# A decoder layer's first token block: read from a transposed copy of x, and finer first conditioning chunks

## The chip, the cores and the metric

The kernel runs on one core of a Trainium2 chip. The metric is the device time of one execution in microseconds, the median of three runs. A core has five engines with a queue of instructions each: TensorE (PE: matmuls, with weight loads PEld beside them), VectorE (DVE), ScalarE (ACT), GpSimd (POOL) and SyncE (SP), which here issues the DMA transfers. Each engine works through its own queue in order and waits at an instruction until what it needs is there.

## The reference

One hybrid decoder layer over 2048 tokens of width 1024, conditioned by a vector c:

```python
mod = jax.nn.silu(c) @ w_ada + b_ada
sh1, sc1, ga1, sh2, sc2, ga2 = jnp.split(mod, 6, axis=-1)
h = modulate(rms_norm(x, g_attn), sh1, sc1)          # x/rms * g * (1 + sc1) + sh1
x = x + ga1[:, None, :] * hybrid_mixer(h, w_in, b_f, sinks, w_out)
h2 = modulate(rms_norm(x, g_mlp), sh2, sc2)
x = x + ga2[:, None, :] * conv_glu_mlp(h2, w_up, conv_w, conv_b, w_down)
return rms_norm(x, g_final)
```

The mixer multiplies h by w_in (q, k, v of a sliding-window group and of a forgetting-attention group, and its gate logits), runs both attentions, and multiplies by w_out. What matters here is the first line and the first part of the third: before anything can be multiplied by w_in, the shift sh1 and the scale sc1 (each 1024 numbers) must come out of `silu(c) @ w_ada`, and x must be divided by its root mean square.

## The kernel before

Tokens are taken in four blocks of 512. For each block there are stages: s1 (h and the input projection), s2 (attention) and s3 (output projection and MLP). Precision: each float32 operand is split into a high and a low part of a reduced format (hh and hl for h, wh and wl for a weight, line 384 and 385 make the latter), and each product is three matmuls, wh·hh, wh·hl and wl·hh. h is held transposed: tile k has 128 of the 1024 features on the partitions and 512 tokens along the row, k from 0 to 7.

The first block has a prologue of its own, since weights, conditioning and x all arrive at the same time.
- `prep(0)` (lines 562 to 577) loads x in rows, four tiles of 128 tokens in two halves of 512 features (line 510). ScalarE sums the squares (line 491), GpSimd forms the inverse root (lines 495 and 496), VectorE scales the rows (line 568).
- `first_groups` (from line 242) first transposes the scaled rows with TensorE (line 517) and copies each of the eight transposed tiles out of PSUM (line 252).
- The conditioning is computed in four chunks of 256 shift and 256 scale columns, enough for two k each. A chunk is eight tiles of w_ada of 128x512, loaded at line 200; VectorE multiplies each by an entry of silu(c) and adds it up (lines 205 and 207). `shape` then sums over the partitions with small matmuls against ones (line 262) and forms shift and scale (lines 267 to 269).
- `modulate_one` makes h for one k: ScalarE applies scale and shift (line 525), ScalarE rounds to hh (line 115), VectorE takes hl (line 530).
- `products` (line 282) multiplies: seven groups of 128 output columns (four q groups, accumulators "d", and three k groups, accumulators "acc") are accumulated over all eight k, three matmuls each, so 21 matmuls for one k and 168 in all. The weights come as sets: for each pair of k one set for the q groups (128x1024) and one for the k groups (128x768), eight sets, numbered 0 to 7. `feed(loads, splits)` issues loads up to a number (line 425) and splits sets up to a number. From inside `products` it runs ahead and reaches sets 8 and 9, which belong to what follows the block. Weight tiles raw, high and low share ten buffers.
- `store_group` (lines 583 to 586) writes the finished groups to memory; the loads of sets 10 and 11 are issued ahead of it by code that stands behind it.

What sets the order: the kernel is written in a language whose planner orders each engine's instructions by priority (program order) and by its own simulated clock, and puts in all waits. Around `first_groups` the order of VectorE and SP is written by hand: those instructions keep their program order among themselves, though instructions from outside can be planned in between. TensorE and ScalarE are ordered by the planner. The loop in `first_groups` is woven: while chunk i is being summed on VectorE, chunk i-1 is shaped after the second step and its two k are modulated and multiplied between later steps; the products with the k groups are put off until the next chunk's column sum has been issued.

Of the kernel before, what the change touches and what calls it, by code (L numbers as in the profile page):

```python
# [8 lines left out]
F32 = mybir.dt.float32  # L9
F32R = mybir.dt.float32r  # L10
BF16 = mybir.dt.bfloat16
AF = mybir.ActivationFunctionType
ALU = mybir.AluOpType
AX = mybir.AxisListType

P = 128
D = 1024
S = 2048
TB = 512
NB = S // TB  # L20
KT = D // P
# [4 lines left out]
EPS = 1e-6  # L26
BIG = 1e30
NT = 10
# [23 lines left out]
MMB = 1  # L52
# [19 lines left out]
def tile_decoder_layer(  # L72
    ctx: ExitStack,
    tc: tile.TileContext,
    x: bass.AP,
    c: bass.AP,
    w_ada: bass.AP,
    b_ada: bass.AP,
    g_attn: bass.AP,
    w_in_c: bass.AP,  # L80
# [45 lines left out]
    def side_ps(w=512):  # L126
        t = pa.tile([P, 512], F32, tag="s", name="sd", bufs=3)
        return t[:, :w]
# [59 lines left out]
    def ada_chunk(i, accs):  # L188
        acc = ap.tile([P, 512], F32, tag="act", name="acc")
        for k in range(KT):  # L190
            w = ap.tile([P, 512], F32, tag="act", name="wada")
            with behind():
                nc.sync.dma_start(w, w_ada[i, k])
            ada_step(acc, w, k)
            yield
        accs.append(acc)

    def ada_pair(i, k, acc):
        w = at.tile([P, 2, 256], F32, tag="t", name="wada2", bufs=NT)
        nc.sync.dma_start(w, w_ada[i, k].rearrange("p (s n) -> p s n", s=2))  # L200
        ada_step(acc, w.rearrange("p s n -> p (s n)"), k)

    def ada_step(acc, w, k):
        if k == 0:
            nc.vector.tensor_scalar(acc, w, cc[:, 0:1], 1.0, ALU.mult, ALU.mult)
        else:
            nc.vector.scalar_tensor_tensor(
                acc, w, cc[:, k : k + 1], acc, ALU.mult, ALU.add
            )
# [30 lines left out]
    late = {}  # L240

    def first_groups():
        rows = ready.pop(0)
        xts = []
        for k in range(KT):
            if k % 4 == 2:
                ps = pa.tile([P, 512], F32, tag="o", name="o0")
            else:
                ps = side_ps()
            transposes(ps, rows, k)  # L250
            xt = ap.tile([P, TB], F32, tag="act", name="xt")
            nc.scalar.copy(xt, ps)
            xts.append(xt)
        hh, hl = {}, {}
        acc = [dense_ps() for _ in range(4)]
        for tag, bufs in (("s", 3), ("o", 1), ("s", 3))[:FG]:
            acc.append(pa.tile([P, 512], F32, tag=tag, name="acc0", bufs=bufs))

        def shape(i, a):
            ps = side_ps(4)  # L260
            for j in range(4):
                nc.tensor.matmul(
                    ps[:, j : j + 1], a[:, j * P : (j + 1) * P], ones[:, 0:1],
                    start=True, stop=True,
                )
            js, jc = slice(2 * i, 2 * i + 2), slice(KT + 2 * i, KT + 2 * i + 2)
            nc.vector.tensor_add(mod[:, js], ps[:, 0:2], bada[:, js])
            nc.vector.tensor_add(mod[:, jc], ps[:, 2:4], bada[:, jc])
            nc.vector.scalar_tensor_tensor(
                scl[:, js], mod[:, jc], 1.0, gat[:, js], ALU.add, ALU.mult  # L270
            )

        def products(k, sets):
            a = k % 2
            for m in sets:
                i = NW * (k // 2) + m
                feed(i + 3, i + 2)
                wh, wl = parts[i]
                for g in range(4 * m, min(4 * m + 4, len(acc))):
                    gs = slice((g - 4 * m) * P, (g - 4 * m + 1) * P)  # L280
                    for j, (l, r) in enumerate(((wh, hh), (wh, hl), (wl, hh))):
                        nc.tensor.matmul(  # L282
                            acc[g], l[:, a, gs], r[k],
                            start=(k == 0 and j == 0), stop=(k == KT - 1 and j == 2),
                        )
                if a == 1:
                    parts.pop(i)
                    flow["used"] += 1

        prev = None  # L290
        for i in range(5):
            sums = None
            if i < 4:
                sums = ap.tile([P, 512], F32, tag="act", name="acc")
            for k in range(KT):
                if i < 4:
                    ada_pair(i, k, sums)
                if i > 0 and k == 1:
                    shape(i - 1, prev)
                    if i > 1:  # L300
                        for m in range(1, NW):
                            products(2 * i - 4, [m])
                            products(2 * i - 3, [m])
                if i > 0 and k in (3, 5):
                    kk = 2 * (i - 1) + (k - 3) // 2
                    modulate_one(*h_pair(hh, hl, kk), xts[kk], kk, 0, 0)
                    if k == 5:
                        products(kk - 1, [0])
                        products(kk, [0])
            prev = sums  # L310
            if i == 0:
                feed(3, 2)
        for m in range(1, NW):
            products(KT - 2, [m])
            products(KT - 1, [m])
        small_loads()
        for g in range(4):
            store_group(acc[g], q_d[0], 512 + g * P, 0.125)
        for g in range(FG):
            store_group(acc[4 + g], k_d[0], P + g * P, 1.0)  # L320
        return hh, hl

    def prologue_late():
        srcs = [(g_mlp, KT, "gml")]
# [90 lines left out]
    def feed(loads, splits):  # L415
        while flow["loaded"] < min(loads, len(reqs)):
            i = flow["loaded"]
            shape, srcs = reqs[i]
            key, use = mode.get(i, (None, "raw"))
            if use == "load":  # L420
                load_kept(i, shape, key)
            else:
                raws[i] = wp.tile(shape, F32, tag="w", name="wr", bufs=WS)
                for dst, src in srcs:
                    flow["last"] = nc.sync.dma_start(raws[i][dst], src).ins
            flow["loaded"] += 1
        while flow["split"] < min(splits, len(reqs)):
            i = flow["split"]
            key, use = mode.get(i, (None, "raw"))
            if use != "load":  # L430
                parts[i] = split_w(raws.pop(i), reqs[i][0])
                if use == "store":
                    store_kept(parts[i], reqs[i][0], key)
            flow["split"] += 1
# [80 lines left out]
    def transposes(ps, rows, k):  # L515
        for t, row in enumerate(rows):
            nc.tensor.transpose(
                ps[:, t * P : (t + 1) * P],
                row[k // 4][:, (k % 4) * P : (k % 4 + 1) * P], ident,
            )  # L520
        return ps
# [51 lines left out]
    def prep(n):  # L573
        for t in range(4):
            prep_tile(n, t)
# [925 lines left out]
    c_raw = columns_load(c.rearrange("o (k p) -> (o k) p", p=P), KT)  # L1501
    b_raw = columns_load(b_ada.rearrange("(k p) -> k p", p=P), 48)
    g_raw = columns_load(g_attn.rearrange("(k p) -> k p", p=P), KT)
    prep(0)
    cc = columns(None, KT, "cc", c_raw)
    ce = cp.tile([P, KT], F32, tag="ce", name="ce")
    nc.scalar.activation(ce, cc, AF.Exp, scale=-1.0)
# [20 lines left out]
def _laid_out(inputs, np):  # L1528


    def columns(w):
        return w.reshape(KT, P, -1, P).transpose(2, 1, 0, 3)

    def rows(w):
        return w.reshape(-1, 2, P, 2, 512).transpose(3, 0, 2, 1, 4)

    def head(w):
        return w.reshape(KT // 2, 2, P, -1).transpose(0, 2, 1, 3)

    def by_partition(w):  # L1540
        return w.reshape(KT, P, -1).transpose(1, 0, 2)

    out = {}
    for name in _INS:
        a = np.asarray(inputs[name])
        if name == "w_ada":
            first = a[:, : 2 * D].reshape(KT, P, 2, 4, 256).transpose(3, 0, 1, 2, 4)
            rest = a[:, 2 * D :].reshape(KT, P, 8, 512).transpose(2, 0, 1, 3)
            out[name] = np.concatenate([first.reshape(4, KT, P, 512), rest])
        elif name == "w_in":  # L1550
            out["w_in_c"] = columns(np.concatenate([a[:, :640], a[:, 768:1792]], axis=1))
            out["w_in_v0"] = by_partition(np.concatenate([a[:, 640:768], a[:, 1792:1984]], axis=1))
            out["w_in_v1"] = by_partition(a[:, 1984:2312])
            out["w_in_h0"] = head(a[:, 768:1280])
            out["w_in_h1"] = head(a[:, 1280 : 1280 + FG * P])
        elif name in ("w_out", "w_down"):
            out[name] = rows(a)
        elif name == "w_up":
            out[name] = columns(a)
        else:  # L1560
            out[name] = a
    return {name: np.ascontiguousarray(a) for name, a in out.items()}
# [29 lines left out]
```

## Time and profile before

| | us |
|---|---|
| Median of three runs | 2652.85 |
| Lowest, highest run | 2644.81, 2661.91 |
| Profiled execution, its own time | 2654.82 |
| Its span | 2653.1 |
| TensorE matmul, busy | 2542.7 (96%) |
| Weight loads, busy | 2152.4 (81%) |
| VectorE, busy | 1927.9 (73%) |
| ScalarE, busy | 1457.2 (55%) |

The profile is of one execution. A row of instructions gives its start, its busy time, engine, line of the kernel, operation and tiles, and in brackets the idle time before it and what ended it. "PEclk" and "granted clock" are the share of TensorE's full clock in a stretch. A row of the chain of waits gives start, length and what the chain passes through. A group's row gives its busy time, the mean ns of one, and idle time before it.

### The profile page before, as it was taken

How to read it: one execution, taken by the hardware profiler on the slowest of the kernel's cores; microseconds unless marked ns; L12 is line 12 of the kernel's file. 1: busy time of each engine (PE TensorE's matmuls, PEld its weight loads, DVE VectorE, ACT ScalarE, POOL GpSimd, SP SyncE). 2: the span in 40 equal slices, each digit the busy share in tenths (PEclk: the TensorE clock that was granted, in tenths of full speed). 3: DMA queues.
4: the chain of work that ended last, by engine and by line, in shares of the span. 5: the costliest groups of instructions: out<-in, count | busy, mean ns of one | idle time of the engine just before them, and what ended most of it. 6: DMA issues, size and time to landing. Idle time of an engine off the chain costs nothing.

```text
span 2653.1 us, 38432 instructions
## 1 busy us (share of the span) xinstructions
PE 2542.7 (96%) x12852; PEld 2152.4 (81%) x12852; DVE 1927.9 (73%) x3837; ACT 1457.2 (55%) x3061; POOL 86.1 (3%) x171
## 2 busy tenths in 40 slices
PE   7999989799999999999999999899998999999998
PEld 6888888688887889888888878788787778888887
DVE  6468767889898668788888767888888876344433
ACT  4456664655657676575556665755555665311222
POOL 0001000100000010010000000100000000000000
PEclk9999999799999999999999999999999999999999
DMA  6967679576556876756666799365554467655564
GB/s 230 302 205 251 198 217 331 204 243 205 192 182 224 274 255 215 257 193 246 226 231 235 255 300 320 126 202 184 185 168 144 160 225 260 238 192 190 191 235 177
DMA packets 304770, 588.25 MB, mean 222 GB/s; under 512 B 32188, under 2 KB 137396, under 8 KB 304572
## 3 DMA queue, kind: packets, MB, share of 16 engines
q1 hardware_dynamic: 304572, 585.79, 66.0%
q8 instruction: 102, 1.67, 0.3%
q14 instruction: 96, 0.79, 0.1%
HBM read 440.95 MB, written 144.71 MB: 221 GB/s over the span
## 4 chain that ended last, share of the span: by engine, by line
PE 83%; DVE 6%; DMA 5%; ACT 3%; issue 1%; SPq 1%; POOL 1%; POOLq 0%; DVEq 0%; ACTq 0%
PE d L1297 36%; PE d L1179 21%; PE d L619 8%; PE s L964 4%; PE d L647 3%; PE o L1062 2%; PE o L1059 2%; PE d L282 1%; PE s L794 1%; PE mb L996 1%; PE pt L836 1%; DVE t L1010 1%; DMA zrow<-zd 1%; DMA wr<-in_w_in_c_dram 1%; DMA wada<-in_w_ada_dram 1%
## 5 line engine op out<-in xcount | busy, mean ns | idle before, releaser
L1297 PE MATMUL d<-hh,wkh 128*128 128x512 f32 (+1 forms) x920 | 353.0, 386 | 3.9 <-ACT hh L115 2.3
L1297 PE MATMUL d<-hl,wkh 128*128 128x512 f32 (+1 forms) x920 | 354.2, 385 | 0.6 <-DVE hl L530 0.6
L1297 PE MATMUL d<-hh,wkl 128*128 128x512 f32 (+1 forms) x920 | 352.9, 384 | 0.0
L385 DVE TENSOR_TENSOR wl<-wr,wh 128x1024 fp32r<-128x1024 f32 (+5 forms) x184 | 219.3, 1193 | 75.6 <-ACT wh L384 73.8
L384 ACT CAST wh<-wr 128x1024 fp32r<-128x1024 f32 (+5 forms) x184 | 188.5, 1026 | 154.8 <-PE d L1297 60.2
L981 ACT ACTIVATE t<-s,bc 128x256 f32<-128x256 f32 (+3 forms) x464 | 200.4, 482 | 130.0 <-PE s L964 62.8
L1327 ACT ACTIVATE u<-d,cb,cw 128x512 f32<-128x512 f32 x176 | 136.3, 778 | 200.5 <-PE d L1297 180.1
L1330 DVE SCALAR_TENSOR_TENSOR u<-d,cw,u 128x511 f32<-128x511 f32 x176 | 130.9, 745 | 149.4 <-ACT u L1327 148.6
L724 ACT CAST ph<-t 128x512 fp32r<-128x512 f32 (+2 forms) x304 | 176.5, 590 | 114.0 <-PE o L1059 113.1
L725 DVE TENSOR_TENSOR pl<-t,ph 128x512 fp32r<-128x512 f32 (+2 forms) x304 | 193.5, 650 | 28.9 <-ACT ph L724 28.3
L1297 PE MATMUL d<-hh,wh 128*128 128x512 f32 (+1 forms) x552 | 211.9, 385 | 1.2 <-ACT hh L115 0.7
L1297 PE MATMUL d<-hl,wh 128*128 128x512 f32 (+1 forms) x552 | 212.2, 385 | 0.0
L1297 PE MATMUL d<-hh,wl 128*128 128x512 f32 (+1 forms) x552 | 211.8, 384 | 0.0
L964 PE MATMUL s<-q,kkb 128*128 128x256 f32 (+2 forms) x1024 | 196.0, 309 | 8.7 <-ACT t L981 4.7
L1297 PEld LDWEIGHTS d<-hh,wkh 128*128 128x128 f32 x920 | 174.1, 190 | 36.5 <-ACT hh L115 3.1
L1297 PEld LDWEIGHTS d<-hh,wkl 128*128 128x128 f32 x920 | 174.5, 190 | 31.6
L1297 PEld LDWEIGHTS d<-hl,wkh 128*128 128x128 f32 x920 | 174.5, 190 | 31.3 <-DVE hl L530 1.1
L1015 ACT ACTIVATE t<-t 128x512 f32<-128x512 f32 (+2 forms) x304 | 170.0, 602 | 15.5 <-DVE t L1014 11.6
L964 PEld LDWEIGHTS s<-q,kkb 128*128 128x128 f32 x1024 | 152.7, 195 | 21.5 <-ACT t L981 7.2
L1062 PE MATMUL o<-pl,vvb 128*128 128x256 f32 (+2 forms) x512 | 147.0, 306 | 19.4 <-DVE pl L725 19.2
L1059 PE MATMUL o<-ph,vvb 128*128 128x256 f32 (+2 forms) x512 | 150.1, 309 | 11.7 <-ACT ph L724 5.6
L619 PE MATMUL d<-hh,wh 128*128 128x512 f32 x360 | 142.8, 400 | 4.7 <-DVE lf L662 3.8
(233 smaller groups left out, 6073.6 us busy)
## 6 DMA issues: line engine op xcount, KB each, us to landing
wkh<-wsu SPq DMA_DIRECT2D x110, 512.0 KB, 3.3
wkl<-wsu SPq DMA_DIRECT2D x110, 512.0 KB, 4.2
wr<-in_w_up_dram SPq DMA_DIRECT2D x66, 512.0 KB, 4.7
wkh<-wsd SPq DMA_DIRECT2D x55, 512.0 KB, 4.2
wkl<-wsd SPq DMA_DIRECT2D x55, 512.0 KB, 4.2
wada<-in_w_ada_dram SPq DMA_DIRECT2D x96, 256.0 KB, 5.7
wr<-in_w_in_c_dram SPq DMA_DIRECT2D x45, 512.0 KB, 4.3
wsu<-wh SPq DMA_DIRECT2D x44, 512.0 KB, 3.0
```

Of the source, the lines that this page charges most:

```text
L384: nc.scalar.copy(wh, raw)
L385: nc.vector.tensor_sub(wl, raw, r32(wh))
L619: nc.tensor.matmul(ps, a[:, k, :], b[k], start=(k == 0 and i == 0), stop=(k == KT - 1 and i == 2),)
L724: nc.scalar.copy(ph[:, e0:], src[:, e0:])
L725: nc.vector.tensor_sub(pl[:, e0:], src[:, e0:], r32(ph[:, e0:]))
L964: nc.tensor.matmul(ps[:, o + low(c0) : o + w], st["kks"][kb // 4][:, (kb % 4) * P : (kb % 4 + 1) * P], qs[a][:, low(c0) : w], start=(a == ...
L981: nc.scalar.activation(tt[:, plain : o + w], ps[:, plain : o + w], AF.Identity, bias=bias(kb))
L1015: nc.scalar.activation(t1, t1, AF.Exp)
L1059: nc.tensor.matmul(po[:, c:], v, ph[:, o + c : o + w], start=(kb == 0), stop=False)
L1062: nc.tensor.matmul(po[:, c:], v, pl[:, o + c : o + w], start=False, stop=(kb == nkb - 1))
L1179: nc.tensor.matmul(acc[t], l[:, ts], r[:, k % 2, :], start=(i == 0 and l is ah and r is wh), stop=(i == n_k - 1 and l is al),)
L1297: nc.tensor.matmul(ps[:, c], w[a][:, k, :], b[k][:, c], start=(k == 0 and i == 0), stop=(k == KT - 1 and i == 2),)
```

## The change

- The host lays out a second input, `x_t`: the first 512 tokens of x transposed, eight tiles of 128 features by 512 tokens. A new function `prep_columns` loads these tiles and takes the place of `prep(0)`: ScalarE squares each, VectorE adds the squares up, TensorE sums over the partitions, GpSimd forms the inverse roots, and TensorE and ScalarE spread them over all partitions as the tile `rsb`. The transposes of rows and the copies of their results are gone from `first_groups`.
- h is now made by `modulate_t`: VectorE multiplies the xT tile by scale and `rsb`, ScalarE adds the shift and rounds to hh in one pass, VectorE takes hl with one more operation (x plus shift minus hh).
- The first two k get a conditioning chunk each. Such a chunk is four loaded tiles, each of which holds two row blocks of 128 shift and 128 scale columns, so eight steps of half width; the other three chunks cover two k each as before. The same 32 tiles of 256 KB are loaded.
- The loop is not woven any more: for each chunk, all of its sums, its shaping, its modulation, a `feed` that splits the chunk's weight sets, and all its products follow one another in program order. Loads run ahead: `load()` keeps up to ten w_ada tiles on order, and issues the weight sets' loads between them. Sets 8 and 9 are no longer loaded from inside the block.
- In `products`, the wl·hh matmuls of four groups now follow the wh·hh and wh·hl matmuls of these groups.

```diff
     def first_groups():
-        rows = ready.pop(0)
-        xts = []
-        for k in range(KT):
...
-            transposes(ps, rows, k)
-            xt = ap.tile([P, TB], F32, tag="act", name="xt")
-            nc.scalar.copy(xt, ps)
-            xts.append(xt)
+        xts, rsb = ready.pop(0)
...
+        chunks = [(0,), (1,), (2, 3), (4, 5), (6, 7)]
+        tiles, todo = [], []
+        for i, ks in enumerate(chunks):
+            todo += [(i, j) for j in range(4 * len(ks))]
+            if i != 1:
+                todo.append(NW * (max(i - 1, 0) + 1))
+
+        def load():
+            while todo and (isinstance(todo[0], int) or len(tiles) < NT):
+                item = todo.pop(0)
+                if isinstance(item, int):
+                    feed(item, 0)
+                    continue
+                i, j = item
+                w = at.tile([P, 512], F32, tag="t", name="wada2", bufs=NT)
+                nc.sync.dma_start(w, w_ada_s[i, j] if i < 2 else w_ada[i - 2, j])
+                tiles.append(w)
+
+        def columns_of(i):
+            ks = chunks[i]
+            n, k0 = len(ks), ks[0]
+            a = ap.tile([P, 512], F32, tag="act", name="acc")[:, : 256 * n]
+            for j in range(4 * n):
+                w = tiles.pop(0)
+                if n == 2:
+                    ada_step(a, w, j)
+                else:
+                    ada_step(a, w[:, 0:256], 2 * j)
+                    ada_step(a, w[:, 256:512], 2 * j + 1)
+                load()
+            ps = side_ps(2 * n)
...
+        def modulate_t(ks):
+            for k in ks:
+                xt, (h, _) = xts[k], h_pair(hh, hl, k)
+                nc.vector.scalar_tensor_tensor(
+                    xt, xt, scl[:, k : k + 1], rsb, ALU.mult, ALU.mult
+                )
+                nc.scalar.activation(h, xt, AF.Identity, bias=mod[:, k : k + 1])
+            for k in ks:
+                nc.vector.scalar_tensor_tensor(
+                    hl[k], xts[k], mod[:, k : k + 1], r32(hh[k]), ALU.add, ALU.subtract
+                )
...
+        load()
+        for i, ks in enumerate(chunks):
+            columns_of(i)
+            modulate_t(ks)
+            feed(0, NW * (ks[0] // 2 + 1))
+            for k in ks:
+                products(k, 0)
+            for m in range(1, NW):
+                for k in ks:
+                    products(k, m)
         small_loads()
...
+    def prep_columns():
+        xts = []
+        for k in range(KT):
+            xt = ap.tile([P, TB], F32, tag="act", name="xt")
+            nc.sync.dma_start(xt, x_t[k])
+            xts.append(xt)
+        total = at.tile([P, TB], F32, tag="acc", name="xsum", bufs=ACB)
+        for k, xt in enumerate(xts):
+            sq = total if k == 0 else tp.tile([P, TB], F32, tag="t", name="xsq")
+            nc.scalar.activation(sq, xt, AF.Square, scale=D ** -0.5)
+            if k > 0:
+                nc.vector.tensor_add(total, total, sq)
+        ps = side_ps(4)
+        for t in range(4):
+            nc.tensor.matmul(
+                ps[:, t : t + 1], total[:, t * P : (t + 1) * P], ones[:, 0:1],
+                start=True, stop=True,
+            )
+        rs = sp.tile([P, 4], F32, tag="nm4", name="rs4")
+        nc.vector.tensor_scalar(rs, ps, EPS, None, ALU.add)
+        nc.gpsimd.tensor_tensor(rs, rs, mhalf, ALU.pow)
+        ps = side_ps()
+        for t in range(4):
+            nc.tensor.transpose(
+                ps[:, t * P : (t + 1) * P], rs[:, t : t + 1].to_broadcast([P, P]), ident
+            )
+        rsb = at.tile([P, TB], F32, tag="mm", name="rsb", bufs=MMB)
+        nc.scalar.copy(rsb, ps)
+        ready[0] = xts, rsb
...
-    prep(0)
+    prep_columns()
```

More of the change, by code (lines that the diff above doesn't have):

```diff
@@ L75, in tile_decoder_layer @@
     x: bass.AP,
+    x_t: bass.AP,
     c: bass.AP,
     w_ada: bass.AP,
+    w_ada_s: bass.AP,
     b_ada: bass.AP,
@@ L192, in ada_chunk @@
             with behind():
-                nc.sync.dma_start(w, w_ada[i, k])
+                nc.sync.dma_start(w, w_ada[i - 1, k])
             ada_step(acc, w, k)
@@ L196, in ada_chunk @@
         accs.append(acc)
[L198 to L201, printed above, removed]
     def ada_step(acc, w, k):
@@ L242, in first_groups @@
     def first_groups():
-        rows = ready.pop(0)
-        xts = []
-        for k in range(KT):
[L246 to L249, printed above, removed]
-            transposes(ps, rows, k)
-            xt = ap.tile([P, TB], F32, tag="act", name="xt")
-            nc.scalar.copy(xt, ps)
-            xts.append(xt)
+        xts, rsb = ready.pop(0)
         hh, hl = {}, {}
@@ L257, in first_groups @@
             acc.append(pa.tile([P, 512], F32, tag=tag, name="acc0", bufs=bufs))
-        def shape(i, a):
-            ps = side_ps(4)
-            for j in range(4):
+        chunks = [(0,), (1,), (2, 3), (4, 5), (6, 7)]
[27 more added lines that the diff above has]
+            ps = side_ps(2 * n)
+            for j in range(2 * n):
                 nc.tensor.matmul(
@@ L265, in shape @@
                 )
-            js, jc = slice(2 * i, 2 * i + 2), slice(KT + 2 * i, KT + 2 * i + 2)
-            nc.vector.tensor_add(mod[:, js], ps[:, 0:2], bada[:, js])
-            nc.vector.tensor_add(mod[:, jc], ps[:, 2:4], bada[:, jc])
+            js, jc = slice(k0, k0 + n), slice(KT + k0, KT + k0 + n)
+            nc.vector.tensor_add(mod[:, js], ps[:, 0:n], bada[:, js])
+            nc.vector.tensor_add(mod[:, jc], ps[:, n : 2 * n], bada[:, jc])
             nc.vector.scalar_tensor_tensor(
@@ L271, in shape @@
             )
-        def products(k, sets):
-            a = k % 2
[L275 to L312, printed above, removed]
@@ L313, in first_groups @@
-        for m in range(1, NW):
-            products(KT - 2, [m])
-            products(KT - 1, [m])
+        def modulate_t(ks):
[9 more added lines that the diff above has]
+                )
@@ new lines, in products @@
+        def products(k, m):
+            i = NW * (k // 2) + m
+            wh, wl = parts[i]
+            gs = range(4 * m, min(4 * m + 4, len(acc)))
+            cut = [slice((g - 4 * m) * P, (g - 4 * m + 1) * P) for g in gs]
+            a = k % 2
+            for g, c in zip(gs, cut):
+                nc.tensor.matmul(acc[g], wh[:, a, c], hh[k], start=(k == 0), stop=False)
+                nc.tensor.matmul(acc[g], wh[:, a, c], hl[k], start=False, stop=False)
+            for g, c in zip(gs, cut):
+                nc.tensor.matmul(acc[g], wl[:, a, c], hh[k], start=False, stop=(k == KT - 1))
+            if a == 1:
+                parts.pop(i)
+                flow["used"] += 1
@@ L1546, in _laid_out @@
         if name == "w_ada":
-            first = a[:, : 2 * D].reshape(KT, P, 2, 4, 256).transpose(3, 0, 1, 2, 4)
+            first = a[:, : 2 * D].reshape(KT, P, 2, 4, 256).transpose(3, 0, 1, 2, 4)[1:]
+            fine = a[:, : 2 * D].reshape(KT // 2, 2, P, 2, KT, P).transpose(4, 0, 2, 1, 3, 5)
+            out["w_ada_s"] = fine[:2].reshape(2, KT // 2, P, 512)
             rest = a[:, 2 * D :].reshape(KT, P, 8, 512).transpose(2, 0, 1, 3)
-            out[name] = np.concatenate([first.reshape(4, KT, P, 512), rest])
+            out[name] = np.concatenate([first.reshape(3, KT, P, 512), rest])
         elif name == "w_in":
@@ L1555, in _laid_out @@
             out["w_in_h1"] = head(a[:, 1280 : 1280 + FG * P])
+        elif name == "x":
+            out["x"] = a
+            out["x_t"] = a[0, :TB].T.reshape(KT, P, TB)
         elif name in ("w_out", "w_down"):
```

## The prediction

> **What bounds the kernel now.** I read the page first, for the span and for where the clock is low, then the windows of the stretch that the change touches, then the chain of waits through it.
>
> ```profile
> core 0 of [0], span 2653.1 us
> ```
> ```profile
> PE 2542.7 (96%) x12852; PEld 2152.4 (81%) x12852; DVE 1927.9 (73%) x3837; ACT 1457.2 (55%) x3061; POOL 86.1 (3%) x171
> ```
> ```profile
> 25.60:74.10 48.50, 45.85 (x193) 37.76 (x194) 31.24 (x51) 18.13 (x28) 0.00 (x0) 0.93 0.52 171
> ```
>
> The last row is a window: length, busy time and instructions of PE, PEld, DVE, ACT and POOL, then granted clock, DMA share, GB/s. It is the first token block's q and k products. PE is busy for 45.85 of 48.5 us; VectorE 31.24. The whole edit lies ahead of 74.1 us, 2.8% of the span, so a large part of the stretch would have to go for 1% to move. The chain of waits there (start, us, what):
>
> ```profile
> 25.67 2.08 PE d L282 x4
> 27.74 0.43 PE acc L282
> 28.17 3.54 PE d L282 x12
> 31.71 0.68 PE acc L282 x3
> ...
> 47.85 0.80 PE sd L262 x8
> 48.68 0.16 DVE mod L267
> 48.94 0.17 DVE scl L269
> 49.13 1.52 ACT hraw L525 x2
> 50.65 0.53 ACT hh L115
> 51.22 2.07 PE d L282 x4
> 53.30 1.28 PE acc L282 x3
> 54.58 3.97 PE d L282 x12
> 58.55 0.68 PE acc L282 x3
> 59.23 1.81 PE d L282 x8
> ```
> ```profile
> 73.85 0.39 PE L282 MATMUL acc<-hh,wl 128*128 128x512 f32 x1
> 74.08 0.39 PE L619 MATMUL d<-hh,wh 128*128 128x512 f32 x1
> ```
>
> The first products start at 25.67 and the next group (L619) at 74.08. Eight matmuls take 1.81 us when the clock is up: 0.226 each, and the 168 of this stretch (8 k times 21) 38.0. From 25.67 to 31.71 seventeen take 6.04 instead of 3.84: 2.2 lost to a low clock. Column sums (L262) cost 0.80, three of them 2.4. Once, from 48.65 to 51.22, PE has nothing: 2.57; and the nineteen matmuls after it take 7.33 instead of 4.3: 3.0 more. 25.67 + 38.0 + 2.2 + 2.4 + 2.57 + 3.0 = 73.8, against 74.1 seen. So the stretch is a late start plus PE's own work; only one gap opens, since half of the previous chunk's products (the k groups) stand behind the column sum in PE's order and cover it.
>
> ```profile
> DVE mod L267 <- PE sd L262: 13.7, 3, 5.2
> ```
>
> VectorE pays for that order: three times it waits for the column sum, 13.7 us in total, and it does not matter, since PE is the later one.
>
> **The change, part by part.** *Start.* Taken away: eight row scalings on VectorE, 32 transposes, eight copies out of PSUM. Added: eight squares on ScalarE, seven adds, four column sums, POOL's power, four transposes, a copy, and a three-operand scaling of each xT tile.
>
> ```profile
> 4.77 5.58 DMA xrow<-in_x_dram
> 10.43 0.63 ACT junk L491 x2
> 11.11 0.73 ACT junk L491 x2
> 11.93 0.31 POOL rs L495
> 12.31 0.57 POOL rs L496
> ```
> ```profile
> 13.70 0.48 DVE L205 TENSOR_SCALAR acc<-wada,cc 128x512 f32<-128x512 f32 x1
> 14.22 5.47 DVE L207 SCALAR_TENSOR_TENSOR acc<-wada,cc,acc 128x512 f32<-128x512 f32 x7
> ```
> ```profile
> L207 DVE SCALAR_TENSOR_TENSOR acc<-wada,cc,acc 128x512 f32<-128x512 f32 x28 | 21.0, 750 | 0.7
> L530 DVE TENSOR_TENSOR hl<-hraw,hh 128x512 fp32r<-128x512 f32 x8 | 5.4, 687 | 1.7 <-ACT hh L115 1.7
> L385 DVE TENSOR_TENSOR wl<-wr,wh 128x1024 fp32r<-128x1024 f32 x4 | 4.9, 1224 | 0.2 <-ACT wh L384 0.2
> L385 DVE TENSOR_TENSOR wl<-wr,wh 128x768 fp32r<-128x768 f32 x4 | 3.8, 952 | 0.0
> ```
>
> The same 2 MB of x lands by about 11.1, when the last square starts. It ends at 11.7, the last add (0.69, as L530) at 12.4. After that the way over PE, POOL (0.57) and ScalarE to the broadcast factors is some 3.8 us, to 16.2. Meanwhile VectorE sums chunk 0: eight steps of half width.
>
> ```profile
> L947 DVE TENSOR_TENSOR mx<-mx,t 128x256 f32<-128x256 f32 x32 | 13.4, 419 | 0.1
> ```
>
> A half-width step is not in the trace. The nearest row from below is this two-operand one, 0.42; from above the full-width step, 0.75. I take 0.42 plus the 0.06 by which L207 exceeds L530: 0.48, and 0.33 for the first step, so 3.7 a chunk. A full-width chunk is 6.0 (13.70 to 19.69). The four tiles land behind x, by 13.3; sums begin between 12.4 and 13.6 and end at 16.7, give or take 0.6.
>
> *From the sum to the first product.* Four column sums 0.40, the three small shaping steps 0.45 (48.65 to 49.11), VectorE's scaling 0.75 (as L207), ScalarE's h.
>
> ```profile
> L525 ACT ACTIVATE hraw<-xt,mod,scl 128x512 f32<-128x512 f32 x8 | 6.1, 807 | 21.9 <-DVE scl L269 21.9
> L115 ACT ACTIVATE hh<-hraw 128x512 fp32r<-128x512 f32 x8 | 4.5, 614 | 0.0
> ```
>
> h has one per-partition operand where L525 has two and L115 none: between 0.61 and 0.81, I take 0.71. With hops of 0.05 that is 2.45, and 2.85 for a chunk with eight column sums. First product: 16.7 + 2.45 = 19.15, against 25.67. This 6.5 us is the gain. It holds only one k, though: 21 matmuls where a chunk before brought 42.
>
> *The loop.* Now all products of a chunk stand ahead of the next column sum in PE's order, and VectorE's order, written by hand, is: scale, low part of h, split of two weight sets (1.22 + 0.95, 2.1 as they follow each other), next sum. C is the time at which a chunk's column sum starts.
> - Chunk 0, C = 16.7: PE from 19.15, 21 matmuls 4.75, cold 2.2, done at 26.1. VectorE: low part done at C + 3.15, splits 5.25, sum 8.95. PE is later: chunk 1 at 26.1.
> - Chunk 1: PE 28.55 to 33.3. VectorE: low part at 29.25, no split, six us of sum: 35.3. PE waits for it.
> - Chunk 2, C = 35.3: PE from 38.15, 42 matmuls 9.5, to 47.65. VectorE: two scalings to C + 2.8, low parts 4.35, splits 6.45, sum 12.45: 47.75. A dead heat.
> - Chunk 3 at 47.75, chunk 4 at 60.2, its products 63.05 to 72.55.
>
> That is 1.5 us ahead of 74.1: 19.15 is 6.5 earlier, the former gap and its low clock (2.57 and 3.0) are gone, and against that stand four gaps of 2.05 without PE work (8.2), the 2.0 that PE waits for chunk 2's sum, and 0.4 for one more set of column sums.
>
> *The clock in these gaps.* Each gap is about 2.05 us idle, 2.9 with its column sum; the one ahead of chunk 2 is 4.85 with it (33.3 to 38.15). The gap of 2.57 idle, 3.4 with the sum, lowered the clock. A shorter one did not:
>
> ```profile
> 102.58 0.39 PE L647 MATMUL d<-wh,hh 128*128 128x328 f32 x1 [2.30 <-DVE vst L659]
> ```
> ```profile
> 100.00:105.00 5.00, 2.70 (x18) 2.47 (x18) 1.36 (x2) 2.10 (x3) 0.00 (x0) 1.00 0.94 328
> ```
>
> 2.30 idle, clock 1.00 throughout. So chunk 2 pays for certain; chunks 1, 3 and 4 lie between the two rows, an even chance each. A drop cost 3.0; where part of the slow time falls into the gap it costs less, I take 2.5. Chunk 1 has 2.0 us of slack, which leaves 0.5. Sum: -1.5 + 2.5 + 0.25 + 1.25 + 1.25 = +3.7 us.
>
> The Trainium skill ("TensorE: Matmul & The Clock Gate", section "HAM oscillation — how this bites in real kernels") speaks of idle gaps above about 3.4 us, the length of one free-running window, as those that halve the clock. By that only the gap ahead of chunk 2 would pay, and the sum would be +1.0; this case's 2.57 us gap dropped nonetheless, so a gap below the page's length can do it, and the measured row stands in my sum.
>
> *What else moves.* Sets 0 to 7 are now all that the block feeds; set 8 and 9's loads and set 8's split pass to the first weights() behind it. Cover: SP issues loads of the code behind the block ahead of the block's stores already:
>
> ```profile
> 64.75 5.92 SPq L425 DMA_DIRECT2D wr<-in_w_in_v_dram  x2
> 70.82 0.33 SPq L585 DMA_DIRECT2D qd<-qh  x1
> ```
>
> By the number of their buffers (ten, of which two chunks' sets hold eight) they can go from about chunk 3 on, 10 us or more ahead of need. I cost it at nothing. Behind 74 us PE is full to 91, so the shift passes on one to one. A scale step less on ScalarE and no transposes cost nothing: neither bounds the stretch.
>
> The profiled execution took 2654.8 us (span 2653.1), the median of the runs is 2652.85: on that scale 2652.85 + 3.7 = 2656.6. Its own range: everything early, half steps at 0.42 and no drop that costs, -2.5; half steps at 0.75 (+3.3), late x (+0.6), three drops at 3.0 and one us at chunk 1, +12.4.
>
> **Rivals.**
> - *The gaps stay warm.* Only chunk 2 pays: +1.0, 2653.9. For it the 2.30 us row; against it the 2.57 one. Chance 0.20.
> - *The early start is kept whole.* If PE never waits for VectorE, the stretch ends 6.5 us earlier: 2646.3. Against it: VectorE's fixed order of 12.45 us a chunk; for it, that VectorE was idle 13.7 us in the stretch. Chance 0.08.
> - *The weight loads come late.* If SP's order puts sets 8 and 9 behind the block's fourteen stores, PE waits for set 8 at the end of the block: landing 6.2, a cast of 1.0, a cold clock 3.0, so +10 on top of +3.7, 2666.8; it decides as soon as the load is issued less than 7 us before the last product. Against it the two SP rows above. Slower than before, chance 0.12.
>
> ```profile
> wr<-in_w_in_c_dram SPq DMA_DIRECT2D x4, 512.0 KB, 6.2
> ```
>
> - *The planner orders the rest anew.* Everything behind the block is placed by a planner that counts time from its start; its order can come out otherwise, either way. 1% is 26.5 us, a quarter of what PE idles in the whole span (busy 2542.7 of 2653.1). Chance 0.10, of which 0.03 faster and 0.05 slower by over 1%.
>
> **How the numbers follow.** Forecast (some gaps drop, 2656.6) 0.50, rivals 0.20, 0.08, 0.12, 0.10. All but the last stay within 1%, which is about what a measurement here can tell from no change: the runs shown lie between 2644.81 and 2661.91. The range takes the lowest run less 2.5 and the highest plus 12.4: 2642 to 2674. Faster by over 1%: 0.03 and 0.01 for the measurement; slower 0.05 and 0.02, the late loads adding to a slow set of runs; within 1%: 0.89.
>
> **What would show it.** First L282-like product near 19 (18 to 21), column sums near 17, 26, 35, 48 and 60, the last product near 73 to 78. Gaps of about 2 us in PE behind each column sum, and a clock below 1.00 in one to four of them. VectorE's waits for the column sum well under 13.7. The w_in_c load issued ahead of the first q store. I am wrong if the column sums come ahead of a chunk's last products, if xT's factors are later than the sum of chunk 0, or if a group behind 74 us waits for weights.

## The result, and the profile after

The changed kernel takes 2667.87 us (median of eight runs, 2663.88 to 2679.91) against 2653.21 us for the kernel before in the same series: 1.0058 times as long, with a 95% interval of 1.0045 to 1.007. That is a loss of 14.7 us, against 3.7 forecast: inside the range and within the one per cent that the forecast gave most weight, but four times the forecast's loss. The profiled execution of it took 2666.64 us, 11.8 us more than that of before. The other 3 us lie in the spread of executions: the profiled one of before took 1.6 us more than its median, that of the changed kernel 1.2 us less.

The page of the changed kernel:

```profile
core 0 of [0], span 2664.9 us
PE 2544.6 (95%) x12832; PEld 2155.1 (81%) x12832; DVE 1938.9 (73%) x3856; ACT 1447.3 (54%) x3038; POOL 84.6 (3%) x164
```

PE does the same work, 2 us more by busy time. Where the span grew is read from windows that are cut where the next group of products starts (L619 before, L658 after). The kernel before, then the changed one, columns as in the prediction:

```profile
0.00:74.08 74.08, 56.59 (x236) 46.20 (x236) 46.68 (x86) 34.19 (x59) 6.20 (x19) 0.95 0.65 223
74.08:2653.10 2579.02, 2486.07 (x12618) 2106.18 (x12616) 1881.25 (x3753) 1423.05 (x3003) 79.88 (x152) 0.98 0.66 222
```
```profile
0.00:85.60 85.60, 55.40 (x215) 44.98 (x216) 57.02 (x104) 24.74 (x35) 3.28 (x12) 0.92 0.57 192
85.60:2664.90 2579.30, 2489.24 (x12618) 2110.15 (x12616) 1881.84 (x3754) 1422.60 (x3004) 81.30 (x152) 0.98 0.67 222
```

The block ends at 85.60 instead of 74.08, 11.5 us later; all that follows takes 2579.3 against 2579.0. So the loss between these two executions arises in the first 86 us, where VectorE now has 57.0 us of work instead of 46.7 and PE is idle for 30 us instead of 17.5. The chain of waits of the changed kernel, up to its first product:

```profile
12.13 1.88 PE sd L346 x8
14.28 1.05 POOL rs L352
15.37 1.12 PE sd L355 x4
16.49 0.74 PE sd L182 x3
17.97 0.37 DVE acc L202
18.36 0.50 DVE acc L204
...
22.02 1.03 PE sd L277 x4
23.53 0.76 DVE xt L291
24.32 0.73 ACT hh L294
```

The first step of chunk 0's sum (L202) starts at 17.97, not between 12.4 and 13.6. Ahead of it stand the norm's small matmuls (L346, L355), POOL's power, and then L182. L182 transposes the raw vectors c, b_ada and g_attn into columns; silu(c), by which each step multiplies, is made from it. In the kernel before the same transposes (its L180) ran as soon as c had landed, as PE's timeline of before shows:

```profile
2.41 0.24 PE L180 MATMUL sd<-ident,colraw 8*128 8x8 f32 x1 [2.41 <-DMA colraw<-in_c_dram]
```

In the changed kernel the load of c was the first that SP issued, at 0.79, but the transposes stood behind the norm's matmuls in PE's queue. PE waited at the first of these until x was squared and added up, at 12.13, and 4.4 us more passed until L182; VectorE's sum waited for silu(c). PE's timeline of the changed kernel at the column sums (L277) and first products (L307):

```profile
25.09 2.07 PE L307 MATMUL d<-hh,wh 128*128 128x512 f32 x4 [2.05 <-ACT hh L294]
32.29 0.50 PE L277 MATMUL sd<-ones,acc 128*128 128x1 f32 x4
34.84 1.19 PE L307 MATMUL d<-hh,wh 128*128 128x512 f32 x4 [2.05 <-ACT hh L294]
41.53 1.05 PE L277 MATMUL sd<-ones,acc 128*128 128x1 f32 x8 [1.62 <-DVE acc L204]
44.64 2.08 PE L307 MATMUL d<-hh,wh 128*128 128x512 f32 x4 [2.06 <-ACT hh L294]
57.07 0.95 PE L277 MATMUL sd<-ones,acc 128*128 128x1 f32 x8
60.07 1.49 PE L307 MATMUL d<-hh,wh 128*128 128x512 f32 x4 [2.05 <-ACT hh L294]
71.36 0.95 PE L277 MATMUL sd<-ones,acc 128*128 128x1 f32 x8
74.36 2.03 PE L307 MATMUL d<-hh,wh 128*128 128x512 f32 x4 [2.05 <-ACT hh L294]
```

Behind each column sum PE has nothing for 2.05 us, the gap that was forecast. Four products in 2.0 us are products at half clock, in 1.19 nearly at full. The first products of all, at 25.09, are slow as in the kernel before. Behind chunk 1's gap the clock held; behind those of chunks 2, 3 and 4 it fell. The windows agree:

```profile
45.00:50.00 5.00, 5.00 (x13) 3.84 (x13) 4.93 (x7) 2.02 (x3) 0.00 (x0) 0.50 0.44 167
60.00:65.00 5.00, 4.93 (x15) 3.92 (x16) 4.88 (x7) 2.35 (x4) 0.00 (x0) 0.66 0.03 2
75.00:80.00 5.00, 5.00 (x18) 3.98 (x17) 4.91 (x7) 2.64 (x3) 0.00 (x0) 0.71 0.00 0
```

What a drop costs is read from the PE rows: 42 products should take 9.5 us. They took 57.07 - 44.64 = 12.4, then 11.3, then 85.60 - 74.36 = 11.2: losses of 2.9, 1.8 and 1.7 us. VectorE's wait for the column sums fell, but only from 13.7 to 10.4 us, and SP issues the w_in_c load ahead of the first q store (qd), as in the kernel before:

```profile
DVE mod L282 <- PE sd L277: 10.4, 5, 4.1
```
```profile
67.97 0.33 SPq L464 DMA_DIRECT2D wr<-in_w_in_c_dram  x1
83.03 0.70 SPq L624 DMA_DIRECT2D qd<-qh  x1
```

### The profile page after: what moved, and what is told of

Read it like the earlier page. It is cut to its first block, busy times and chain, and to the rows that moved or that the text cites. A ratio compares the mean times of both kernels' runs of the same rounds, so it can differ in the third digit from the quotient of the medians.

```text
span 2664.9 us, 38388 instructions
## 1 busy us (share of the span) xinstructions
PE 2544.6 (95%) x12832; PEld 2155.1 (81%) x12832; DVE 1938.9 (73%) x3856; ACT 1447.3 (54%) x3038; POOL 84.6 (3%) x164
## 4 chain that ended last, share of the span: by engine, by line
PE 81%; DMA 6%; DVE 6%; ACT 4%; issue 1%; SPq 1%; POOL 1%; POOLq 0%; DVEq 0%; ACTq 0%
PE d L1336 36%; PE d L1218 20%; PE d L658 7%; PE s L1003 4%; PE d L686 3%; PE o L1101 2%; PE o L1098 2%; DMA q<-qd 1%; PE mb L1035 1%; DVE t L1049 1%; DMA wr<-in_w_in_c_dram 1%; PE d L556 1%; PE s L833 1%; DMA yraw<-yd 1%; ACT t L1054 1%
## 5 line engine op out<-in xcount | busy, mean ns | idle before, releaser
L1098 PE MATMUL o<-ph,vvb 128*128 128x256 f32 (+2 forms) x512 | 151.0, 311 | 11.7 <-ACT ph L763 5.6
L658 PE MATMUL d<-hh,wh 128*128 128x512 f32 x360 | 143.2, 401 | 4.0 <-DVE lf L701 3.9
```

The lines of the kernel that those rows point to most:

```text
L658: nc.tensor.matmul(ps, a[:, k, :], b[k], start=(k == 0 and i == 0), stop=(k == KT - 1 and i == 2),)
L1098: nc.tensor.matmul(po[:, c:], v, ph[:, o + c : o + w], start=(kb == 0), stop=False)
```

## The experiments

Two causes offer themselves: the late start of chunk 0's sum, and the low clock behind the gaps. The first three runs undo them one at a time and together; the others ask what the parts of the change are worth, and whether a better order is to be had. "Measured" gives first the time as a ratio to the kernel before in the same series, with its 95% interval (the changed kernel: 1.0058 [1.0045, 1.007]). "Ends" is where the next group of products starts in the profiled execution (after: 85.60; before: 74.08).

**The transposes of c first.** The call is moved, nothing else:

```diff
-    prep_columns()
     cc = columns(None, KT, "cc", c_raw)
...
     gat = columns(None, KT, "gat", g_raw)
+    prep_columns()
```

> The kernel after, with one move: silu(c), the bias and g columns are written ahead of the xT prologue, so that their small transposes no longer stand behind the norm's matmuls in PE's order. Theory (the first conditioning sum was late because it waited for silu(c), not for x or its tiles): the first half-width step moves from 17.97 us to about 13, the first column sum from 22.0 to about 17, and the next group behind the block from about 85.6 to about 80.6; the whole about 5 us less than the kernel after, a ratio to before near 1.004. Rival (xT's broadcast factors, ready at 17.1, hold the start anyway): the first scaling moves by less than 1.5 us and the block's end with it.

Measured: 1.003 [1.0016, 1.0044], ends at 78.74. VectorE's and PE's timelines of this version:

```profile
11.54 0.35 DVE L202 TENSOR_SCALAR acc<-wada,cc 128x256 f32<-128x256 f32 x1
```
```profile
2.43 1.09 PE L182 MATMUL sd<-ident,colraw 8*128 8x8 f32 x3 [2.43 <-DMA colraw<-in_c_dram]
16.86 0.85 PE L277 MATMUL sd<-ones,acc 128*128 128x1 f32 x4
19.84 2.07 PE L307 MATMUL d<-hh,wh 128*128 128x512 f32 x4 [2.13 <-ACT hh L294]
29.20 1.54 PE L307 MATMUL d<-hh,wh 128*128 128x512 f32 x4 [2.05 <-ACT hh L294]
```

With c first the sum starts at 11.54, the column sum stands at 16.86 (forecast 16.7) and the first product at 19.84 (19.15). The later column sums are at 26.54, 35.89, 50.30 and 64.54, against 26.1, 35.3, 47.75 and 60.2 without drops. So the place of one call is worth 6.9 of the 11.5 us in the block (behind it this version takes 2581.4, 2.1 more than the changed kernel; no run here says why). What remains, 4.7 us over the end of before, is the loop as the forecast had it, clock drops included.

**The gaps kept warm.** Eight matmuls by a tile of zeros are issued behind each column sum from chunk 1 on; they add nothing to the result.

```diff
+            if k0 > 0:
+                with tc.issue_after(last.ins):
+                    for _ in range(8):
+                        nc.tensor.matmul(acc[0], zeros, hh[k0 - 1], start=False, stop=False)
```

> The kernel after, plus eight matmuls by a tile of zeros (they add nothing to the accumulator) behind each column sum from the second chunk on, 1.8 us of PE work in each gap of 2.05 us. Theory (what the gaps cost beyond their own length is TensorE's lowered clock, 2.9, 1.8 and 1.9 us behind chunks 2, 3 and 4): the clock stays at 1.00 behind chunks 3 and 4, possibly also behind 2, and the block ends 3.5 to 6.5 us earlier (82 to 79 instead of 85.6). Rival (the clock falls for another reason, or the gap's own length is all): the block ends at 85.6 or later, and 32 matmuls of 0.226 to 0.43 us are added where they delay the products.

Measured: ends at 80.7, 4.9 us earlier, but 1.0068 [1.0043, 1.0093] in the runs. The windows of the first products behind the column sums of chunks 2, 3 and 4, which answer to 0.50, 0.66 and 0.71 above:

```profile
45.00:50.00 5.00, 5.00 (x21) 4.01 (x20) 4.89 (x8) 1.94 (x3) 0.00 (x0) 0.85 0.48 172
55.00:60.00 5.00, 4.91 (x26) 3.86 (x25) 3.41 (x8) 2.36 (x4) 0.00 (x0) 1.00 0.62 192
70.00:75.00 5.00, 4.91 (x22) 3.73 (x21) 4.87 (x8) 3.55 (x5) 0.00 (x0) 1.00 0.12 46
```

From 50 us on the clock reads 1.00, so behind chunks 3 and 4 the slow products are the gaps' doing. Behind chunk 2, where PE first waits 1.63 us for VectorE's sum, the clock still fell: the eight matmuls by zeros took 3.11 us there, 2.11 behind the other two. The total did not follow: what stands behind the block took 2582.6 us in this execution, 3.3 more than in the changed kernel. One row of PE's timeline of this version, over 1,100 us behind the block, has no match in the changed kernel:

```profile
1197.33 0.79 PE L1342 MATMUL d<-hh,wkh 128*128 128x512 f32 x1 [3.64 <-DVE halo L1386]
```

This wait comes back below, with the question of how much of the 3.3 us is due to it.

**Both together.** The two edits above in one kernel.

> The kernel after with both single causes taken away: silu(c) first and zero matmuls in the gaps. Theory (late silu(c) and the low clock are what the changed kernel loses to the one before): the savings of the two, 6.9 and 4.9 us in the profiles, add up, the block ends near 74 like the kernel before, ratio 1.000 to 1.002. Rival (they overlap, since an earlier start falls otherwise into the clock's windows): it ends at 77 or later.

Measured: 1.0013 [1.0, 1.0026], median 2656.0, ends at 75.2. The two savings taken alone add up to 11.8; together they gave 10.4, and 1.1 us of the block's loss is left. Here the rest took 2578.9, as before. So these two causes account for some nine tenths of the block's loss, and the two edits together bring the ratio from 1.0058 down to 1.0013.

**No fine chunks.** The changed kernel with four chunks of two k each, silu(c) still late:

```diff
-        chunks = [(0,), (1,), (2, 3), (4, 5), (6, 7)]
+        chunks = [(0, 1), (2, 3), (4, 5), (6, 7)]
```

> The kernel after, with the first two conditioning chunks taken together again (four chunks of two tiles each, all steps full width); transposed x and the unwoven loop stay. Theory (the fine chunks cost more than they bring, since they add a gap and a wait): the first product comes at 27.4 instead of 25.1, but 42 are ready then; column sums near 24, 39, 53 and 68, and the block ends near 82, 3.5 us earlier than after. Rival (the fine chunks do bring the early start): the block ends later than 85.6, by about the 2.3 us of the later first product.

Measured: 1.006 [1.0043, 1.0078], ends at 83.0, 2.6 us ahead of the fine chunks. The first product comes later (27.87 instead of 25.09), but there are four gaps instead of five, and the first brings 42 products. So in this loop, with the late start, the fine chunks did not pay. The rest took 2582.8, again with a wait of 3.62 us for the same halo line.

**The loop without the transposed copy.** x read in rows and transposed on PE as before; the new chunks and the new loop stay.

> The other part alone: x by rows with transposes as before, the changed conditioning chunks and the unwoven loop. Theory (the loop is what costs; with rows the planner puts silu(c) first by itself): first column sum near 17.7, gaps behind each column sum, low clock in two to four of them, the block ends near 79, 5 us behind the kernel before, like e1_c_first. Rival (the transposed copy costs): it ends near 74.

Measured: 1.0039 [1.0024, 1.0055], ends at 83.0. A row of its PE timeline:

```profile
40.56 2.07 PE L308 MATMUL d<-hh,wh 128*128 128x512 f32 x4 [2.58 <-ACT hh L116]
```

Its first product is early (21.03), since silu(c) is early here, yet it ends 9.0 us after the kernel before, 4 us later than expected. ScalarE needs two passes for h, so the gaps are longer (2.02 to 2.58), and behind all three of 2.58 the first four products take 2.07 or 2.08 us, half speed. The loop is the costly part of the change: alone it costs 9.0 us, and the read of x adds 2.6 to it as the change has it and takes off 4.3 where c comes first (78.74). The new place of the wl·hh matmuls is part of this version too; no run takes it alone.

**A woven loop on the transposed copy.** c first, four pair chunks; a chunk's shaping and scaling stand between the next chunk's sum steps, and the products with the k groups behind the next column sum in program order, as in the kernel before.

```diff
+                some(steps, 1)
+                columns_of(i - 1)
+                scale_t(ks)
+                if i > 1:
+                    for m in range(1, NW):
+                        for k in chunks[i - 2]:
+                            products(k, m)
+                some(steps, 2)
+                low_t(ks)
```

> Transposed x alone, with silu(c) first: four chunks of two tiles, and the loop woven again as in the kernel before (the next chunk's sums between shaping and low parts, the products with the k groups behind the next column sum). Theory (the loss lies in the unwoven loop and the late silu(c), not in the transposed copy): sums from about 13, first column sum near 19, first product near 22, then PE's own 38 us, 2 us of low clock and the column sums: the block ends between 64 and 70 us, 4 to 10 us ahead of the kernel before, a ratio to before of 0.996 to 0.999. Rival (the transposed path itself costs, by its adds and three-operand steps on VectorE): the block ends at 74 or later.

Measured: 1.002 [1.0007, 1.0032], ends at 74.36, no better than before.

```profile
47.88 2.08 PE L312 MATMUL d<-hh,wh 128*128 128x512 f32 x4 [2.05 <-ACT hh L297]
61.91 2.08 PE L312 MATMUL d<-hh,wh 128*128 128x512 f32 x4 [2.05 <-ACT hh L297]
```

The planner orders PE's queue, and at the last two column sums it put the k groups ahead: the gap is back, twice, with its low clock. The end is the one that the rival named, but these gaps stand for it, not the transposed path; the next run tests that.

**The order bound.** The same, and those products may not be issued before the column sum:

```diff
+                    with tc.issue_after(summed[0]):
                         for m in range(1, NW):
```

> Transposed x, silu(c) first, four chunks of two tiles, woven loop, and an explicit order on TensorE: the products with the k groups of a chunk are issued behind the next chunk's column sum. Theory (what is left of the loss in e2_woven_pairs are the two gaps of 2.05 us where the planner put those products ahead of the column sum, with their low clock): no gap above 2 us with nothing to do behind a column sum, clock 1.00 from the second chunk on, first product near 22.6, the block ends between 66 and 69, 5 to 8 us ahead of the kernel before; ratio 0.997 to 0.999. Rival (VectorE's order sets the chunks' pace whatever TensorE does): column sums stay 13 to 14 us apart and the block ends near 74.

Measured: ends at 68.6, 5.5 us ahead of the kernel before, with a clock of 1.00 in every window from 30 us on; 0.9996 [0.9987, 1.0006] in the runs, so no difference that can be told from none. The block came out as expected, the ratio of 0.997 to 0.999 did not show. The column sums are 12.6, 11.6 and 11.7 us apart, not 13 to 14, and the transposed path is no loss in itself.

```profile
42.30 1.02 PE L280 MATMUL sd<-ones,acc 128*128 128x1 f32 x8 [0.81 <-DVE acc L203]
53.97 1.02 PE L280 MATMUL sd<-ones,acc 128*128 128x1 f32 x8 [0.85 <-DVE acc L203]
```

What PE waits for now is VectorE's sum, 11.67 us a chunk.

**The same with fine chunks.** Besides the chunks, the low parts come one step of the next sum earlier.

> The same as e7_forced_pairs with the fine chunks of the changed kernel (first two k one chunk each). Theory (fine chunks bring the first product 2.8 us earlier, near 19.8, but TensorE then has 12 matmuls to do and waits for the second chunk, and VectorE does 1.4 us more): the block ends within 2 us of e7_forced_pairs. Rival (the early start counts): 2 to 3 us ahead of it.

Measured: 1.0005 [0.9995, 1.0015], ends at 73.0, 4.4 us later than with pairs, so neither expectation came true.

```profile
21.05 0.79 PE L314 MATMUL d<-hh,wh 128*128 128x512 f32 x1 [3.07 <-ACT wh L449]
33.42 1.05 PE L282 MATMUL sd<-ones,acc 128*128 128x1 f32 x8 [2.37 <-DVE acc L204]
```

The first column sum is 0.9 us earlier than with pairs (17.13, 18.04), but then the first product waits for the weights' high part. Between the second and the third column sum PE has 21 products (chunk 0's k groups and chunk 1's q groups), too few to cover a pair's sum: it waits 2.37 us.

**The order bound in the kernel before.** x in rows, the old loop, and only that one wait added.

> The kernel before with one thing changed: the products of a chunk's k groups are bound to be issued behind the next chunk's column sum, in every chunk. If the order on PE is what the faster versions live from, the gap of 2.57 us behind the third column sum and the low clock behind it (3.0 us) go: the block ends near 74.1 - 5.6 = 68.5, the ratio is near 0.998. If the transposed read is needed for the gain, the block stays within 2 us of 74.1, because another gap opens in place of the one removed.

Measured: ends at 69.54, 4.5 us ahead of before. In the kernel before the planner had put chunk 1's k groups ahead of the third column sum, though program order has them behind it, and so opened its gap. Here the column sums stand at 34.04, 44.51 and 54.98 with no idle time before them, and the 2.57 us gap and its low clock are gone: 4.5 of the 5.6 us came. The transposed copy with the same order ends 0.9 us earlier. Yet the runs gave 1.0017 [1.0006, 1.0028], and behind the block the profiled execution took 2582.5 us, 3.4 more than before. PE's and VectorE's timelines of this version show the wait met twice above:

```profile
1182.72 0.79 PE L1298 MATMUL d<-hh,wkh 128*128 128x512 f32 x1 [3.64 <-DVE halo L1342]
```
```profile
1176.98 3.69 DVE L1011 TENSOR_TENSOR t<-t,mm 128x512 f32<-128x512 f32 x6
...
1181.32 1.21 DVE L386 TENSOR_TENSOR wl<-wr,wh 128x1024 fp32r<-128x1024 f32 x1
1182.46 0.20 DVE L1342 SCALAR_TENSOR_TENSOR halo<-d,cw,halo 128x1 f32<-128x1 f32 x1
```

The planner has put six other steps and a weight split ahead of the small halo step on VectorE, and PE waits for that. Three of the twelve versions, before and after among them, have this wait, of 3.62 to 3.64 us each time; the other nine have none there. That it is as long in three executions points to the order that a version got, not to chance.

But this wait is not the whole account. Two other waits of PE are in all twelve versions, one of 5.15 or 5.16 us and one of 3.96 or 3.97, and cut the rest into parts. The kernel before, then this version:

```profile
1151.02 0.66 PE L996 MATMUL mb<-ident,rl 128*128 128x128 f32 x2 [5.16 <-ACT ph L724]
1674.00 0.55 PE L1059 MATMUL o<-ph,vvb 128*128 128x256 f32 x1 [3.96 <-ACT t L1015]
```
```profile
1138.79 0.66 PE L997 MATMUL mb<-ident,rl 128*128 128x128 f32 x2 [5.16 <-ACT ph L725]
1671.83 0.55 PE L1060 MATMUL o<-ph,vvb 128*128 128x256 f32 x1 [3.96 <-ACT t L1016]
```

From the block's end to the first of them it is 1076.9 us before and 1069.3 here, 7.7 less; from there to the second 523.0 and 533.0, 10.1 more, of which the halo wait is 3.6. With the gaps kept warm the two parts are 4.3 us less and 6.3 more than before, without fine chunks 3.6 less and 7.6 more. So these versions come to that stretch ahead of the kernel before and lose more in it than the one wait; that the difference of the whole rest comes out near the wait's length is in part luck. What else costs there, and why a change at the start leads to that order here and not there, stays open.

**A warm start.** The pairs with the order bound, and nine matmuls by zeros ahead of the first product (four behind the norm's column sums, five behind the first chunk's); they add nothing to the result.

> The forced pairs, with nine added matmuls by a tile of zeros ahead of the first product (four behind the norm's column sums, five behind the first chunk's column sum; they add nothing to the result). If the slow first products (2.2 us lost) come only from a low clock, the first product stays within 0.5 us of 22.0, the first 42 products take 9.5 instead of 11 or so, and the block ends near 66.5, 2 us ahead of the forced pairs without them (68.6). If the matmuls of zeros delay the column sum or the factors, the first product is later by 1 to 2 us and the block ends near 68.6 again.

Measured: ends at 68.43 against 68.6; 0.9993 [0.9983, 1.0003], median 2649.17. The profiled execution, 2643.46, was the shortest of its series: behind the block it took 2573.3 us, 5.7 less than the one of before, and no run here says why.

```profile
21.91 2.07 PE L318 MATMUL d<-hh,wh 128*128 128x512 f32 x4
23.92 1.88 PE L319 MATMUL d<-hl,wh 128*128 128x512 f32 x4
25.72 1.21 PE L321 MATMUL d<-hh,wl 128*128 128x512 f32 x4
30.49 1.02 PE L280 MATMUL sd<-ones,acc 128*128 128x1 f32 x8 [0.81 <-DVE acc L203]
```

The first product is not delayed, but the first eight are as slow as without zeros; the third four take 1.21 us instead of 2.00. And PE then waits 0.81 us for VectorE's sum, so faster products gain next to nothing (0.2 us). Neither expectation was right: the slow first products cost next to nothing where VectorE sets the pace. No version here beats the kernel before by more than the runs can tell.

## Why the prediction was right and wrong

- **Where the time is** was right: the rest behind the block is equal to 0.3 us, and the loss is one of the block. That equality is a sum, though: up to the common wait of 5.15 us (1161.41) the changed kernel's rest is 1.1 us shorter, behind it 1.4 longer.
- **The start was wrong**, and this is the step that failed: "sums begin between 12.4 and 13.6". It took silu(c) as given, because in the trace of before the transposes of c ran at 2.41. But the change emits norm matmuls ahead of the transposes of c, and on PE they came first. Column sum 0 came at 22.02 instead of 16.7. Every PE instruction that the new function issues should have been set against what already stood in PE's queue behind it; the prediction did this for SP's queue only. Moved back, the forecast's 16.7 came out at 16.86, which is partly luck: the sum began at 11.54, ahead of the forecast's 12.4 to 13.6, and ended at 16.04, and the column sum then stood behind the norm's four transposes (L355, from 15.95) in PE's queue.
- **A half-width step** was sized at 0.48 and is 0.52 from start to start (18.36 to 18.88 is a row of the chain above and the next); 4.0 us a chunk instead of 3.7. The way from the last add to the broadcast factors took 5.0 us (12.1 to 17.1) instead of 3.8. Small misses.
- **From the sum to the first product** 2.45 and 2.85 were forecast; 3.07 came for the first chunk, 2.55 for the second, and 3.0 to 3.1 for the pairs. The first column sum is slow too: 1.03 for four, not 0.40.
- **The loop** was right: all products ahead of the next column sum, gaps of 2.05, and after the start PE waits for VectorE only at chunk 2's sum (1.62, forecast 2.0).
- **The clock** was right in kind and low in total. One to four drops were forecast, and chunk 2, said to be sure, was one of three. They cost 2.9, 1.8 and 1.7, in all 6.4 against the 5.25 in the sum: chunks 3 and 4, counted by half, both dropped, each for less than the 2.5 assumed.
- **The sum.** The block's end was forecast at 74.1 + 3.7 = 77.8. It is 7.8 later: 5.3 from the start, 0.9 between the first two column sums (first products at half speed, slower shaping), -0.2 for chunk 1, and 0.6 for each of the three pairs. With c first the end is 78.74, 0.9 over the forecast. That the measured time lies in the range all the same is luck: the 12.4 us at its upper end stand for slower half-width steps, late x and full clock drops, and none of them for a silu(c) that comes late.
- **The rivals.** "The gaps stay warm" fell: three did not. The Trainium skill's page "TensorE: Matmul & The Clock Gate", section "HAM oscillation — how this bites in real kernels", by which only gaps over about 3.4 us count, would have given one drop (4.7 us from the last product ahead of chunk 2 to the next); 2.05 us without any work, 3.0 with the column sum, were enough here. "The early start is kept whole" fell with the start. "The weight loads come late" fell by the two SP rows: 67.97 is ahead of 83.03. "The planner orders the rest anew" adds only 0.3 us to this result, but over the versions the rest takes from 5.7 us less (with the warm start) to 3.8 more (without fine chunks) than in the kernel before, one profiled execution each, within the one per cent. What the prediction did not see as a rival is that PE's order would change at the start itself.

## What to carry to other kernels

When a new step is put ahead of an old one in program order, look on every engine's queue for what it now stands ahead of; three tiny transposes behind a norm cost 6.9 us of the block here, and moving one call gave them back. An order that keeps PE busy across another engine's work is best bound outright: a few lines removed a gap in the old kernel as well as in the new, and gave most of what the new read of x could in the block. A gain of 5 us at the start of a 2650 us program can be gone behind the part that was edited, so cut the trace where the edit ends, and again at waits that both versions have, and compare the parts before naming one wait as the cause.

## What the runs showed of the hardware

- No single length of gap separates warm from cold. From a column sum's start to the next product, 2.55 us kept the clock (34.84, changed kernel) and 2.66 lowered it (29.20 in the version with c first); the changed kernel's three of 3.0 and more behind chunks 2 to 4 all lowered it. Yet 2.30 us of plain idle time kept it (102.58, kernel before). In the fine chunks with the order bound, 0.98 us idle and a column sum of 1.02 (56.80) were followed by products at 0.63 us each instead of 0.39; with pairs, 0.85 and 1.02 were not. The Trainium skill's page "TensorE: Matmul & The Clock Gate", section "Part 1: The HAM clock gate (the "warmup" mystery)", says that the gate watches windows that run free of the program; an overlap of lengths like this one would fit that, and no run here tests it.
- Matmuls by zeros can hold the clock: behind chunks 3 and 4 the windows read 1.00 with them, 0.66 and 0.71 without. Behind chunk 2, after a wait of 1.63 us, they did not: 0.81 and 0.85 from 40 to 50 us, against 0.87 and 0.50 without.
- At the start of a program the granted clock in the records can't be relied on. The first four products take the same 2.07 or 2.08 us, whether the record reads 1.00 (before, 26 to 32 us) or 0.50 (the old loop with the order bound, 25 to 30 us). There the durations tell.
